# A two-layer encoder in split float32: the gated ConvFFN's convolution and product put off by a few weight units, and more units of the down projection's second chunk ahead of the first chunk's last ones

## The chip, the cores and the metric

One core of a Trainium2 chip runs the whole program. The metric is the device time of one execution in microseconds (us), as the median of several runs. The core has a matrix engine (TensorE, PE in the profile, with its weight loads as PEld), a vector engine (VectorE, DVE), a scalar engine (ScalarE, ACT), a general engine (GpSimd, POOL) and an engine that mainly issues transfers (SyncE, SP; SPq, POOLq and so on are the queues from which transfers are issued).

## The reference

Two layers work on 256 tokens of width 2048 in float32. Layer 0 mixes the tokens with dilated sliding-window attention and differential attention, layer 1 with grouped-query attention and two-dimensional neighbourhood attention. After each mixer comes a gated ConvFFN, and at the end one RMSNorm. The change touches the ConvFFN only:

```
y    = rmsnorm(h, gain)                  # 256 x 2048
gate = y @ w_gate                        # 256 x 5632
up   = y @ w_up                          # 256 x 5632
gate = conv over 3 neighbouring tokens(gate) + bias   # per channel
h    = h + (gelu(gate) * up) @ w_down    # 5632 -> 2048
```

## The kernel before

**Weights.** All weights come from HBM as units of 128 rows x 1024 columns (512 KB). SP issues the load of a unit into one of five `raw` buffers. A product keeps float32 accuracy by three passes: a unit is split into a high part `wh` (a cast on ACT, L234) and a low part `wl` (a subtraction on DVE, L237), and PE multiplies wh by the activation's high part, wl by the high part, and wh by the low part (L198 to L200, L890). There are four `wh` and four `wl` buffers. An ordinary unit is 12 matmuls. Some units go in pairs as blocks, with fewer products: both raw units are loaded (L907, L908), four sums on DVE form new operands (L911, L912, L915, L918), and these are split too; `form` is a fourth operand. The merges at L870 to L875 put the results of the blocks together in the accumulators (`sum`, `gm`, `s`, `tp`).

**ConvFFN.** The 5632 channels are taken in 11 up groups of 512: six in the first half (`HALVES`, groups 0 to 5, `g0 = 0`), five in the second (groups 6 to 10, `g0 = 6`). An up group is two chunks: the gate (x = 0) and the up projection (x = 1). When a chunk's products are done, `done` scales them out of the accumulators into `z` (ACT, L980) and transposes z in squares (DVE, L282). Sixteen transfers of 32 KB then move z to its place in a `qk` tile (L276): four of them are issued by SP and twelve by POOL. When the gate has been moved, `convolved` runs in two parts, each of two 128-channel blocks: a scaled copy on ACT (L1003), two multiply-adds on DVE (L1004, L1006), and a gelu on ACT (L1009). When the up chunk has been moved, `multiplied` forms the product (DVE, L1036) and splits it into `prod`, and for some groups into sums for blocks of the down projection. After each half, the down projection multiplies `prod` by that half's rows of `w_down`: four chunks of 512 columns, taken two and two (c = 0, then c = 2). Their results are added into h (L388), and in the second half squares for the next norm are taken. In layer 1's second half `finish_all` does this.

**What sets the order.** `two_chunks` runs the units of two chunks. `ahead` and `spots` say at which (chunk, unit) the blocks of the next group are loaded. `mixed` changes the order of units: the first chunk stops short of its last `mixed` units, then `mixed` units of the second chunk run, then the first chunk's last ones, then the rest. After every second unit comes a `tick`. `later(delay, fn)` puts fn on a list, and it runs at the tick that is `delay` ticks on; so delays count pairs of weight units. A scheduler then orders the instructions of each engine, by what is ready, in part ahead of their place in the program. Each engine takes its instructions strictly in its own order: what stands behind a waiting instruction waits too.

Of the kernel before, what the change touches and what calls it, by code (L numbers as in the profile page):

```python
# [74 lines left out]
def trunk_kernel(ctx: ExitStack, tc, a, out):  # L75
# [21 lines left out]
    def later(delay, fn, rank=2):  # L97

        pending.append((now[0] + delay, rank, fn))
# [464 lines left out]
    ps = tps("s", 2)  # L564
# [404 lines left out]
    def up_group(layer, j, yT, rstd, prod, ready, ahead, spots, *more):  # L969

        sides = {}

        def hook(x, u):
            if not j and not x and u == 2:
                rstd.append(row_factor())

        def done(x, ps):
            z = new_z("f k")
            for t in range(2):
                S.activation(z.rearrange("p (f t) k -> p t f k", t=2)[:, t],  # L980
                             ps[t].rearrange("p (f k) -> p f k", k=P), AF.Copy, scale=rstd[0][:, t:t + 1])
            sides[x] = quad(2 * x)
            turned(z.rearrange("p b k -> p (b k)"), sides[x].rearrange("p f (t k) -> p (f t) k", k=P), (3,))
            if not x:
                for part in range(2):
                    later(part + 3, lambda part=part: convolved(layer, j, sides, part))

        if not j:
            side[0] = 0
            ready = [[tps("gm", 4), tps("gm", 4)] for _ in range(2)], []  # L990
        nxt = two_chunks([a["up"][layer, j, x] for x in range(2)], yT, 8, ready, ahead, spots, done, hook)
        later(3, lambda: multiplied(j, sides, prod, *more))
        return nxt

    def convolved(layer, j, sides, part):

        if not part:
            sides[2] = quad(4)
        g4, c4 = sides[0], sides[2]
        for i in (2 * part, 2 * part + 1):  # L1000
            f = 4 * j + i
            g, c = g4[:, i, :], c4[:, i, :]
            S.activation(c, g, AF.Identity, scale=convw[:, layer, 1, f:f + 1], bias=convb[:, layer, f:f + 1])  # L1003
            V.scalar_tensor_tensor(c[:, 1:SEQ], g[:, 0:SEQ - 1], convw[:, layer, 0, f:f + 1],  # L1004
                                   c[:, 1:SEQ], op0=ALU.mult, op1=ALU.add)
            V.scalar_tensor_tensor(c[:, 0:SEQ - 1], g[:, 1:SEQ], convw[:, layer, 2, f:f + 1],  # L1006
                                   c[:, 0:SEQ - 1], op0=ALU.mult, op1=ALU.add)
        half = c4[:, 2 * part:2 * part + 2, :]
        S.activation(half, half, AF.Gelu_apprx_tanh)  # L1009
# [34 lines left out]
    def down_front(src, c, act, forms, homes):  # L1044
        return front(src[c:c + 2], act, [2 * n + 1 for n in HALVES[0][2]], forms, homes)

    def ffn(layer, yT, gain, last=False):
        rstd, res, ready = [], None, None
        for g0, g1, seven in HALVES:
            prod, forms = [], {}  # L1050
            nk = 4 * (g1 - g0)
            nu = nk // 2
            src = [a["down"][layer, c, 2 * g0:2 * g1] for c in range(4)]
            for j in range(g0, g1):
                if j + 1 < g1:
                    ahead, spots = (lambda: up_front(layer, j + 1, yT)), [(0, 5 if j == 0 else 3), (1, 5 if j == 0 else 3)]
                    spots = spots[-len(blocks(j + 1)):]
                else:
                    ahead = lambda: down_front(src, 0, prod, forms, ["pt", "pt", "scc"] if g0 else ["act20", "act22", "scc"])
                    spots = [(0, 3), (1, 1), (1, 4)]  # L1060
                ready = up_group(layer, j, yT, rstd, prod, ready, ahead, spots, forms, g0, seven)
            if g0:
                res = [None] * KT
                if last:
                    finish_all(src, prod, forms, nk, ready)
                    return
            for c in (0, 2):
                if not c:
                    ahead, spots = (lambda: down_front(src, 2, prod, forms, ["qk0", "qk2", "qk4"])), [(1, 2), (1, 4), (1, 5)]
                elif not g0:  # L1070
                    ahead, spots = (lambda: up_front(layer, g1, yT)), [(1, 2), (1, 6)]
                else:
                    ahead = None
                ready = two_chunks(src[c:c + 2], prod, nu, ready, ahead, spots, lambda x, ps: finish_chunk(
                    ps, c + x, gain, res, 1 + x if c == 0 else 1), lambda x, u: last_product(c + x, u, nu), 2 if g0 and not c else 0)
        return res

    def last_product(c, u, nu):
        if not c and u == nu - 2:
            flush()  # L1080
# [184 lines left out]
    def finish_all(src, act, forms, nk, ready):  # L1265

        def done(ps, c):
            if not c:
# [5 lines left out]
        nu = nk // 2  # L1274
        load_gains()
        ready = two_chunks(src[0:2], act, nu, ready, lambda: down_front(src, 2, act, forms, ["qk0", "qk2", "qk4"]),
                           [(1, 2), (1, 4), (1, 5)], lambda x, ps: done(ps, x),
                           lambda x, u: last_product(x, u, nu), 2)
        pss, direct = ready[:2]
        for u, s4, t4 in direct:  # L1280
            direct_products(pss, src[2:4], act, u, s4, t4)
# [165 lines left out]
```

## Time and profile before

| | us |
|---|---|
| median of 3 runs | 2431.88 |
| lowest and highest | 2427.51, 2438.07 |
| the profiled execution | 2433.43 |
| its span on the core | 2431.4 |
| PE busy in the span | 2390.6 |
| DVE busy | 1856.6 |
| ACT busy | 1413.3 |
| POOL busy | 540.0 |

The mean granted clock of the profiled execution was 0.998. In its span layer 0's ConvFFN lies at about 660 to 1363 us and layer 1's at about 1715 to 2424 us. A row of the timeline reads: start, duration, engine, line of the kernel, operation, output<-inputs, and in brackets how long the engine was idle before it and what it waited for. A row with x2 stands for two instructions in a row, with the time of both. A row of the waits reads: who waited for whom, us in total, how often, the longest.

### The profile page before, as it was taken

To read this page: it belongs to the slowest core of one execution; us is meant where nothing else is said; L and a number is where in the kernel's file an instruction comes from. 1 tells how busy PE (TensorE), PEld (TensorE's weight loads), DVE (VectorE), ACT (ScalarE), POOL (GpSimd) and SP (SyncE) were. 2 spreads that over 40 slices of the span, in tenths; PEclk is the share of its full clock that TensorE was granted. 3 is DMA by queue.
4 is the path that set the end of the run, shared out by engine and by line. 5 is a ranking of instruction groups with operands and counts; after the bars stand their busy time and mean duration, and the time that the engine had idled before them with its cause. 6 is when DMAs were issued, how large, how long until landed. Compare 5 with 4: busy or idle time off the path is not lost.

```text
span 2431.4 us, 33503 instructions
## 1 busy us (share of the span) xinstructions
PE 2390.6 (98%) x10844; PEld 1972.4 (81%) x10844; DVE 1856.6 (76%) x2525; ACT 1413.3 (58%) x2106; POOL 540.0 (22%) x940
## 2 busy tenths in 40 slices
PE   9999999999999999999999999999999999999998
PEld 7888888888877887788777888888788877888777
DVE  6576567666778997778888667766788977789986
ACT  6455455566656665456666567545566654566654
POOL 1132032321222322012231200322123320033310
PEclk9999999999999999999999999999999999999999
DMA  8678678866777887778888754667688887788875
GB/s 308 202 196 241 198 189 242 222 191 195 214 208 221 250 248 227 228 224 235 246 235 237 239 181 141 193 189 212 189 240 256 236 230 232 224 239 234 246 237 180
DMA packets 296464, 538.19 MB, mean 221 GB/s; under 512 B 160088, under 2 KB 161496, under 8 KB 296288
## 3 DMA queue, kind: packets, MB, share of 16 engines
q1 hardware_dynamic: 265776, 502.66, 66.6%
q0 software_dynamic: 30080, 32.74, 7.8%
q8 instruction: 85, 1.39, 0.2%
q14 instruction: 91, 0.75, 0.1%
q10 hardware_dynamic: 432, 0.66, 0.1%
HBM read 490.99 MB, written 2.18 MB: 203 GB/s over the span
## 4 chain that ended last, share of the span: by engine, by line
PE 68%; DMA 11%; DVE 11%; issue 4%; POOL 2%; ACT 2%; SPq 1%; DVEq 0%; ACTq 0%; POOLq 0%
PE gm L890 15%; PE gm L198 10%; PE gm L199 10%; PE gm L200 10%; PE s L890 9%; PE tp L890 6%; DVE wl L237 5%; DMA qk<-z 5%; DMA raw<-in_down 3%; PE gm L148 2%; DMA raw<-in_up 2%; POOL qk L276 2%; PE gm L153 1%; ACT wh L234 1%; DVE qk L1004 1%
## 5 line engine op out<-in xcount | busy, mean ns | idle before, releaser
L234 ACT CAST wh<-raw 128x1024 fp32r<-128x1024 f32 (+1 forms) x922 | 927.5, 1018 | 695.7 <-PE gm L200 249.8
L237 DVE TENSOR_TENSOR wl<-raw,wh 128x1024 fp32r<-128x1024 f32 (+1 forms) x922 | 1075.8, 1180 | 325.2 <-ACT wh L234 316.5
L276 POOL DMA_DIRECT2D qk<-z x656 | 378.5, 585 | 1148.5 <-DVE z L282 1073.1
L199 PE MATMUL gm<-wl,yT 128*128 128x512 f32 x988 | 385.1, 390 | 1.7 <-DVE wl L237 1.7
L198 PE MATMUL gm<-wh,yT 128*128 128x512 f32 x988 | 386.6, 392 | 0.0
L200 PE MATMUL gm<-wh,yT 128*128 128x512 f32 x988 | 385.0, 390 | 0.0
L890 PE MATMUL gm<-wh,yT 128*128 128x512 f32 x1040 | 332.9, 390 | 0.0
L890 PEld LDWEIGHTS gm<-wh,yT 128*128 128x128 f32 x1040 | 195.5, 188 | 40.9
L199 PEld LDWEIGHTS gm<-wl,yT 128*128 128x128 f32 x988 | 185.7, 188 | 39.5 <-DVE wl L237 2.4
L200 PEld LDWEIGHTS gm<-wh,yT 128*128 128x128 f32 x988 | 185.5, 188 | 39.0
L198 PEld LDWEIGHTS gm<-wh,yT 128*128 128x128 f32 x988 | 185.6, 188 | 37.9 <-ACT junk L268 0.4
L890 PE MATMUL gm<-wl,yT 128*128 128x512 f32 x520 | 203.7, 392 | 2.2 <-DVE wl L237 2.2
L890 PE MATMUL s<-wh,yT 128*128 128x512 f32 x568 | 184.5, 390 | 0.0
L890 PE MATMUL gm<-wh,prod 128*128 128x512 f32 (+1 forms) x560 | 177.8, 389 | 1.0 <-ACT wh L234 1.0
L890 PE MATMUL tp<-wh,yT 128*128 128x512 f32 x496 | 156.3, 389 | 0.0
L890 PEld LDWEIGHTS s<-wh,yT 128*128 128x128 f32 x568 | 106.6, 188 | 22.6
L890 PEld LDWEIGHTS gm<-wh,prod 128*128 128x128 f32 x560 | 105.1, 188 | 22.8 <-ACT wh L234 1.4
L890 PEld LDWEIGHTS gm<-wl,yT 128*128 128x128 f32 x520 | 97.7, 188 | 26.4 <-DVE wl L237 5.5
L890 PE MATMUL gm<-wl,prod 128*128 128x512 f32 x280 | 110.1, 393 | 6.1 <-DVE wl L237 6.1
L890 PE MATMUL s<-wl,yT 128*128 128x512 f32 x284 | 111.0, 391 | 0.4 <-DVE wl L237 0.4
L890 PEld LDWEIGHTS tp<-wh,yT 128*128 128x128 f32 x496 | 93.1, 188 | 19.3
L199 PE MATMUL gm<-wl,mix 128*128 128x512 f32 x256 | 100.6, 393 | 2.0 <-DVE wl L237 2.0
(336 smaller groups left out, 3731.1 us busy)
## 6 DMA issues: line engine op xcount, KB each, us to landing
raw<-in_up SPq DMA_DIRECT2D x390, 512.0 KB, 4.9
raw<-in_down SPq DMA_DIRECT2D x200, 512.0 KB, 4.6
raw<-in_eva_qk SPq DMA_DIRECT2D x96, 512.0 KB, 4.3
raw<-in_eva_v SPq DMA_DIRECT2D x46, 512.0 KB, 6.1
qk<-z POOLq DMA_DIRECT2D x656, 32.0 KB, 4.6
raw<-in_evb_qk SPq DMA_DIRECT2D x32, 512.0 KB, 4.8
raw<-in_ev_out SPq DMA_DIRECT2D x32, 512.0 KB, 4.0
raw<-in_od_qk SPq DMA_DIRECT2D x32, 512.0 KB, 4.0
```

The source lines that it names most:

```text
L148: T.matmul(ps.rearrange("p a b -> p (a b)"), wh[:, k * P:(k + 1) * P], act[u * 8 + k].rearrange("p a b -> p (a b)"), start=(u == 0 and k = ...
L153: T.matmul(ps[:, 1, :], wl[:, k * P:(k + 1) * P], act[u * 8 + k][:, 0, :], start=False, stop=(u * 8 + k == KT - 1))
L198: T.matmul(ps[t], ah, wh[:, sl], start=(kt == 0), stop=False)
L199: T.matmul(ps[t], ah, wl[:, sl], start=False, stop=False)
L200: T.matmul(ps[t], al, wh[:, sl], start=False, stop=(kt == nk - 1))
L234: first = S.copy(dst_h, src)
L237: V.tensor_tensor(dst_l, src, dst_h.bitcast(F32), op=ALU.subtract)
L276: (nc.sync if i in on_sync else G).dma_start(dst[j * 32:(j + 1) * 32, :, i * 32:(i + 1) * 32], z[i * 32:(i + 1) * 32].rearrange("p (b j c) ...
L890: T.matmul(ps, x, y, start=first and i == 0, stop=last and i == 2, skip_group_check=onto)
L1004: V.scalar_tensor_tensor(c[:, 1:SEQ], g[:, 0:SEQ - 1], convw[:, layer, 0, f:f + 1], c[:, 1:SEQ], op0=ALU.mult, op1=ALU.add)
```

## The change

Five numbers change:

1. `convolved` runs one tick later (`part + 4` ticks after the gate chunk in place of `part + 3`), and in the first group (j = 0) two ticks later.
2. `multiplied` runs one tick later (4 in place of 3).
3. In the first half, the third block of the down projection's second pair of chunks is loaded one unit later: spot (1, 6) in place of (1, 5).
4. `mixed` for the first pair of down chunks is 2 in the first half (it was 0) and 4 in the second (it was 2).
5. The same 4 in place of 2 in `finish_all`, for layer 1's second half.

```diff
             if not x:
                 for part in range(2):
-                    later(part + 3, lambda part=part: convolved(layer, j, sides, part))
+                    later(part + (4 if j else 5), lambda part=part: convolved(layer, j, sides, part))
...
         nxt = two_chunks([a["up"][layer, j, x] for x in range(2)], yT, 8, ready, ahead, spots, done, hook)
-        later(3, lambda: multiplied(j, sides, prod, *more))
+        later(4, lambda: multiplied(j, sides, prod, *more))
...
                 if not c:
-                    ahead, spots = (lambda: down_front(src, 2, prod, forms, ["qk0", "qk2", "qk4"])), [(1, 2), (1, 4), (1, 5)]
+                    ahead, spots = (lambda: down_front(src, 2, prod, forms, ["qk0", "qk2", "qk4"])), [(1, 2), (1, 4), (1, 5 if g0 else 6)]
...
                 ready = two_chunks(src[c:c + 2], prod, nu, ready, ahead, spots, lambda x, ps: finish_chunk(
-                    ps, c + x, gain, res, 1 + x if c == 0 else 1), lambda x, u: last_product(c + x, u, nu), 2 if g0 and not c else 0)
+                    ps, c + x, gain, res, 1 + x if c == 0 else 1), lambda x, u: last_product(c + x, u, nu), 0 if c else 4 if g0 else 2)
...
                            [(1, 2), (1, 4), (1, 5)], lambda x, ps: done(ps, x),
-                           lambda x, u: last_product(x, u, nu), 2)
+                           lambda x, u: last_product(x, u, nu), 4)
```

Every engine keeps the same instructions; what changes is their order. On PE and POOL the up groups keep theirs. Three places, in the names of the program (a number tells buffers apart; the same work can have another number in the two kernels):

Layer 0, the boundary of groups 0 and 1. ACT, before and then after: `wh<-raw` are casts of weight units, `qk<-qk,convb,convw` is the convolution's first step on the gate of group 0, `sum` and `s` are merges.

```order
L234 CAST wh_6421<-raw_6419 128x1024
L1003 ACTIVATE qk_6437<-qk_6272,convb,convw 128x256 x2
L234 CAST wh_6447<-raw_6445 128x1024
L234 CAST wh_6465<-raw_6463 128x1024
L1009 ACT_TABLE_LOAD
L1009 ACTIVATE qk_6437<-qk_6437 128x512
L870 COPY sum_6481<-s_6380 128x512
L1003 ACTIVATE qk_6437<-qk_6272,convb,convw 128x256 x2
L234 CAST wh_6520<-raw_6518 128x1024
```

```order
L234 CAST wh_6421<-raw_6419 128x1024
L1003 ACTIVATE qk_6554<-qk_6272,convb,convw 128x256
L234 CAST wh_6439<-raw_6437 128x1024
L870 COPY sum_6473<-s_6380 128x512
L234 CAST wh_6457<-raw_6455 128x1024
L234 CAST wh_6505<-raw_6503 128x1024
L1003 ACTIVATE qk_6554<-qk_6272,convb,convw 128x256 x3
L874 COPY s_6381<-sum_6475 128x512
L234 CAST wh_6520<-raw_6518 128x1024
```

The first step of the convolution stays behind the cast of wh_6421, but it stands there once in place of twice; the other three follow after three more casts, and the gelu behind them.

The same boundary on DVE, before and then after: `wl<-raw,wh` are the low parts of weight units, `qk<-qk,convw,qk` the convolution's multiply-adds.

```order
L237 TENSOR_TENSOR wl_6422<-raw_6419,wh_6421 128x1024
L1004 SCALAR_TENSOR_TENSOR qk_6437<-qk_6272,convw,qk_6437 128x255
L1006 SCALAR_TENSOR_TENSOR qk_6437<-qk_6272,convw,qk_6437 128x255
L1004 SCALAR_TENSOR_TENSOR qk_6437<-qk_6272,convw,qk_6437 128x255
L1006 SCALAR_TENSOR_TENSOR qk_6437<-qk_6272,convw,qk_6437 128x255
L237 TENSOR_TENSOR wl_6448<-raw_6445,wh_6447 128x1024
L237 TENSOR_TENSOR wl_6466<-raw_6463,wh_6465 128x1024
L871 TENSOR_TENSOR sum_6482<-sum_6481,tp_6382 128x512
L1004 SCALAR_TENSOR_TENSOR qk_6437<-qk_6272,convw,qk_6437 128x255
L872 TENSOR_TENSOR sum_6483<-sum_6482,s_6381 128x512
```

```order
L237 TENSOR_TENSOR wl_6422<-raw_6419,wh_6421 128x1024
L1004 SCALAR_TENSOR_TENSOR qk_6554<-qk_6272,convw,qk_6554 128x255
L1006 SCALAR_TENSOR_TENSOR qk_6554<-qk_6272,convw,qk_6554 128x255
L237 TENSOR_TENSOR wl_6440<-raw_6437,wh_6439 128x1024
L871 TENSOR_TENSOR sum_6474<-sum_6473,tp_6382 128x512
L237 TENSOR_TENSOR wl_6458<-raw_6455,wh_6457 128x1024
L872 TENSOR_TENSOR sum_6475<-sum_6474,s_6381 128x512
L873 TENSOR_TENSOR tp_6382<-sum_6474,tp_6383 128x512
L875 TENSOR_TENSOR tp_6383<-sum_6475,tp_6383 128x512
L237 TENSOR_TENSOR wl_6506<-raw_6503,wh_6505 128x1024
L237 TENSOR_TENSOR wl_6521<-raw_6518,wh_6520 128x1024
L1004 SCALAR_TENSOR_TENSOR qk_6554<-qk_6272,convw,qk_6554 128x255
```

Ahead of the first weight split behind wl_6422, four multiply-adds have become two; the others follow after four splits.

SP at the end of layer 1's second half's up groups, before and then after: `in_up` and `in_down` are weight units, `qk<-z` the four of the sixteen moves that SP issues.

```order
L131 DMA raw_21007<-in_up 128x1024
L131 DMA raw_21025<-in_up 128x1024
L907 DMA raw_21043<-in_down 128x1024
L276 DMA qk_20919<-z_20916 32x8x32 x4
L908 DMA raw_21044<-in_down 128x1024
L131 DMA raw_21078<-in_up 128x1024
L131 DMA raw_21096<-in_up 128x1024
```

```order
L131 DMA raw_21007<-in_up 128x1024
L131 DMA raw_21025<-in_up 128x1024
L907 DMA raw_21043<-in_down 128x1024
L908 DMA raw_21044<-in_down 128x1024
L276 DMA qk_20898<-z_20895 32x8x32 x4
L131 DMA raw_21078<-in_up 128x1024
L131 DMA raw_21096<-in_up 128x1024
```

The block's second load (L908) has passed the four moves of the gate.

DVE at that end, where the last group but one is multiplied (L1036), before and then after.

```order
L237 TENSOR_TENSOR wl_20844<-raw_20841,wh_20843 128x1024
L237 TENSOR_TENSOR wl_20862<-raw_20859,wh_20861 128x1024
L1036 TENSOR_TENSOR qk_20683<-qk_20683,qk_20694 128x1024
L237 TENSOR_TENSOR wl_20880<-raw_20877,wh_20879 128x1024
L332 TENSOR_TENSOR sums_20897<-qk_20683 128x128
L334 TENSOR_TENSOR sums_20897<-qk_20683 128x128
L333 TENSOR_TENSOR sums_20897<-sums_20897,qk_20683 128x128
L237 TENSOR_TENSOR prod_20904<-qk_20683,prod_20904 128x256
L335 TENSOR_TENSOR sums_20897<-qk_20683,sums_20897 128x128
L237 TENSOR_TENSOR prod_20907<-qk_20683,prod_20907 128x256
L237 TENSOR_TENSOR prod_20910<-qk_20683,prod_20910 128x256
L237 TENSOR_TENSOR prod_20913<-qk_20683,prod_20913 128x256
```

```order
L237 TENSOR_TENSOR wl_20837<-raw_20834,wh_20836 128x1024
L237 TENSOR_TENSOR wl_20862<-raw_20859,wh_20861 128x1024
L911 TENSOR_TENSOR t_3953_20938<-raw_20934 128x512
L237 TENSOR_TENSOR wl_20880<-raw_20877,wh_20879 128x1024
L237 TENSOR_TENSOR wl_20919<-raw_20916,wh_20918 128x1024
L912 TENSOR_TENSOR raw_20934<-raw_20935,raw_20934 128x512
L1036 TENSOR_TENSOR qk_20770<-qk_20770,qk_20686 128x1024
L915 TENSOR_TENSOR raw_20935<-raw_20935,t_3953_20938 128x512
L237 TENSOR_TENSOR wl_20942<-raw_20934,wh_20941 128x1024
L918 TENSOR_TENSOR raw_20935<-raw_20935 128x512
L237 TENSOR_TENSOR wl_20944<-raw_20935,wh_20943 128x512
L237 TENSOR_TENSOR wl_20944<-t_3953_20938,wh_20943 128x512
```

L1036, which waits for the moves of the up chunk, has come behind more weight splits and into the sums of a block; the product's own sums and splits now follow behind the block's splits.

## The prediction

> **What bounds the kernel now.** I read the page's busy line first, then a table of stretches, then the waits, then the timeline at each place where TensorE (PE) stands still. The busy line:
>
> ```profile
> PE 2390.6 (98%) x10844; PEld 1972.4 (81%) x10844; DVE 1856.6 (76%) x2525; ACT 1413.3 (58%) x2106; POOL 540.0 (22%) x940
> ```
>
> PE is busy in 2390.6 of 2431.4 us. The change adds and removes no matmul, so it can only win from the 40.8 us in which PE is idle. The two ConvFFNs, by stretches (length, then busy time of PE, PEld, DVE, ACT and POOL):
>
> ```profile
> 660.00:1363.00 703.00, 688.72 (x3000) 561.37 (x3000) 583.00 (x759) 415.73 (x566) 161.41 (x280) 1.00 0.79 234
> 1715.00:2424.00 709.00, 695.15 (x3032) 565.56 (x3030) 582.16 (x760) 413.40 (x564) 154.50 (x268) 1.00 0.77 230
> ```
>
> PE idles 703.00 - 688.72 = 14.3 us in the first and 709.00 - 695.15 = 13.9 us in the second. The other 12.7 us lie outside the code that the change touches. So 28.1 us are the most that there is to win. Cut closer, with one row for each place where PE stops (length minus PE's busy time is the idle time):
>
> ```profile
> 695.00:715.00 20.00, 18.66 (x81) 14.76 (x80) 15.71 (x22) 12.57 (x18) 1.48 (x3) 1.00 0.62 198
> 750.00:765.00 15.00, 12.20 (x46) 9.33 (x45) 11.54 (x17) 9.51 (x14) 2.78 (x5) 0.89 0.57 188
> 915.00:940.00 25.00, 23.91 (x104) 18.88 (x103) 21.11 (x27) 15.64 (x22) 6.29 (x12) 1.00 0.81 243
> 960.00:985.00 25.00, 22.60 (x99) 17.97 (x98) 21.55 (x28) 9.71 (x13) 0.00 (x0) 1.00 0.67 209
> 1165.00:1200.00 35.00, 33.64 (x147) 27.04 (x146) 31.81 (x48) 21.52 (x33) 11.52 (x21) 1.00 0.73 212
> 1250.00:1290.00 40.00, 37.88 (x159) 29.11 (x158) 37.41 (x53) 24.95 (x37) 11.52 (x20) 1.00 0.79 219
> 1310.00:1340.00 30.00, 26.84 (x115) 21.02 (x114) 27.85 (x38) 18.49 (x30) 4.61 (x8) 1.00 0.76 223
> 1740.00:1760.00 20.00, 18.04 (x78) 14.20 (x77) 16.29 (x23) 13.49 (x19) 3.35 (x6) 1.00 0.58 168
> 1790.00:1805.00 15.00, 14.21 (x62) 11.37 (x61) 12.49 (x19) 9.52 (x14) 1.97 (x4) 1.00 0.65 215
> 1940.00:1985.00 45.00, 40.87 (x173) 31.67 (x172) 37.68 (x50) 27.39 (x38) 10.11 (x19) 1.00 0.79 233
> 2010.00:2025.00 15.00, 13.45 (x59) 10.82 (x59) 12.02 (x17) 6.55 (x9) 0.00 (x0) 1.00 0.61 202
> 2230.00:2240.00 10.00, 9.61 (x43) 7.59 (x42) 8.81 (x13) 7.22 (x11) 2.55 (x5) 1.00 0.65 215
> 2270.00:2330.00 60.00, 56.91 (x243) 44.64 (x242) 52.53 (x72) 38.18 (x55) 17.55 (x31) 1.00 0.83 247
> 2355.00:2375.00 20.00, 18.15 (x79) 14.10 (x78) 18.48 (x25) 11.89 (x18) 0.00 (x0) 1.00 0.63 195
> ```
>
> These are seven sites in each layer, in order: **A** the boundary of up groups 0 and 1 (1.34 and 1.96 us), **B** of groups 1 and 2 (2.80, 0.79), **C** the end of the first half's up groups (1.09, 4.13), **D** the first half's down phase (2.40, 1.55), **E** the first boundary of the second half (1.36, 0.39), **F** the end of its up groups (2.12, 3.09), **G** its down phase (3.16, 1.85). Together 28.0 us. At all other group boundaries PE does not stop.
>
> Who is late there? PE waits for weight splits (L237 on DVE, some L234 on ACT), and the splits stand behind instructions that wait for data (line waited for, us in total, times, longest):
>
> ```profile
> ACT qk L1003 <- DMA qk<-z: 32.1, 16, 4.3
> DVE raw L912 <- DMA raw<-in_down: 20.1, 12, 4.5
> DVE qk L1036 <- DMA qk<-z: 15.0, 12, 3.4
> ```
>
> The convolution's first step (L1003) and the product (L1036) wait for the moves of the transposed z, and the block sums (L912) for a down weight.
>
> **The change, part by part.** No instruction comes or goes; every cost is one of place.
>
> *Sites A and B: a split ahead of the rest of the convolution.* Site A and then site B in the first layer:
>
> ```profile
> 699.17 1.09 ACT L1003 ACTIVATE qk<-qk,convb,convw 128x256 f32<-128x256 f32 x2 [4.06 <-DMA qk<-z]
> 699.81 0.48 DVE L1004 SCALAR_TENSOR_TENSOR qk<-qk,convw,qk 128x255 f32<-128x255 f32 x1 [3.43 <-ACT qk L1003]
> 701.65 2.36 DVE L237 TENSOR_TENSOR wl<-raw,wh 128x1024 fp32r<-128x1024 f32 x2
> 702.92 0.50 PE L199 MATMUL gm<-wl,yT 128*128 128x512 f32 x1 [0.55 <-DVE wl L237]
> ...
> 752.78 1.09 ACT L1003 ACTIVATE qk<-qk,convb,convw 128x256 f32<-128x256 f32 x2 [5.95 <-DMA raw<-in_up]
> 755.29 1.03 ACT L234 CAST wh<-raw 128x1024 fp32r<-128x1024 f32 x1
> 756.37 0.51 PE L890 MATMUL gm<-wh,form 128*128 128x512 f32 x1 [1.13 <-ACT wh L234]
> 757.28 3.49 DVE L237 TENSOR_TENSOR wl<-raw,wh 128x1024 fp32r<-128x1024 f32 x3
> 758.55 0.49 PE L890 MATMUL gm<-wl,form 128*128 128x512 f32 x1 [1.68 <-DVE wl L237]
> ```
>
> At A, the first L1003 keeps its place and its wait, but only one stands ahead of the next cast (two took 1.09 us, so about 0.55 earlier), and two steps of the convolution instead of four ahead of the next split. Four of them fill 699.81 to 701.65, so two are worth 0.9 us. That is more than the 0.55 us that PE waits, and the 0.79 behind it (1.34 - 0.55) stands behind the second pair, which now has three splits ahead of it. I take A from 1.34 to 0, and from 1.96 to 0.3 in the second layer, where the first stop is longer.
> At B the cast of 755.29 comes two L1003 earlier, at about 754.4: 1.13 becomes 0.3. Its split comes behind four convolution steps instead of eight, and may start when its cast ends, at 755.5 instead of 757.28: 1.8 us earlier against 1.68 of wait. So B goes from 2.80 to 0.3, and from 0.79 to 0.
> What is late next: group 0's product L1036 now stands one split earlier. It waits on DVE for the up quarter's moves, and the split behind it waits with it. The longest such wait on the moves is 3.4 us. I charge 1.2 us in the first layer and 0.7 in the second.
>
> *Sites C and F: the block's second load ahead of the moves.* The second layer's C:
>
> ```profile
> 1956.77 2.55 SPq L276 DMA_DIRECT2D qk<-z  x4
> 1959.43 0.54 SPq L908 DMA_DIRECT2D raw<-in_down  x1
> 1965.81 0.69 DVE L912 TENSOR_TENSOR raw<-raw,raw 128x512 f32<-128x512 f32 x1 [4.48 <-DMA raw<-in_down]
> 1967.76 0.50 PE L890 MATMUL gm<-wh,prod 128*128 128x512 f32 x1 [1.02 <-ACT wh L234]
> 1969.14 0.50 PE L890 MATMUL gm<-wl,prod 128*128 128x512 f32 x1 [0.88 <-DVE wl L237]
> ```
>
> SP issues the four moves only when z is transposed, and the load L908 stands behind them; DVE waits 4.48 us for it, and PE 1.02 + 0.88 us for the splits behind it. After the change L908 is issued ahead of the moves, some 3 to 4 us earlier, so these 1.90 us go. The product L1036 stands two splits and a block sum later, which takes off an estimated 0.5 us, and the rest, 1.7 us, stays. C: 1.09 to 0.1, 4.13 to 1.7. At F a like load is waited for, and a first L1003 behind which a split waits now has that split ahead of it: 2.12 to 0.5, 3.09 to 1.0.
>
> *Sites D, E and G: the order of the down units.* Two (first half) or four (second half) units of the second chunk come ahead of the first chunk's last two (now four), so the last products are needed 2 units later on PE, which is just the extra delay given to L1036: no gain for it there. The stops at D and G stand behind block sums whose loads are late, and these load earlier only in the second half. I take a fifth off: D 2.40 to 1.9 and 1.55 to 1.2, G 3.16 to 2.5 and 1.85 to 1.5. At E the splits stand behind one of the twelve waits of L1036, which is now put off by two units: 1.36 to 0.3, 0.39 to 0.
>
> *The quiet boundaries* lose their order too: convolution steps and block sums alternate, and some splits come up to one convolution step (0.48 us) later. One example of the cover:
>
> ```profile
> 843.57 2.35 DVE L237 TENSOR_TENSOR wl<-raw,wh 128x1024 fp32r<-128x1024 f32 x2
> 846.94 0.39 PE L890 MATMUL gm<-wl,form 128*128 128x512 f32 x1
> ```
>
> The first of the two splits ends near 844.79 and PE needs it at 846.94, 2.15 us later. So one step costs nothing there; I charge 0.8 us in all for places with less cover.
>
> **Sum.** A 0.3, B 0.3, C 1.8, D 3.1, E 0.3, F 1.5, G 4.0: 11.3 us of 28.0 stay, a gain of 16.7. Less 1.9 for group 0's product and 0.8 for the quiet boundaries: 14.0. The moves land when z is ready plus their own time, and PE that runs ahead meets the next landing earlier; no row prices that, so its bounds are 0 and the whole gain. The trace has about as many stops that hang on landings as stops that hang on mere order, but the convolution also comes two units later; I take a quarter, 3.5 us. The net gain is 10.5 us. The profiled execution took 2433.43 us, so it becomes 2422.9; the median of the runs, 1.55 lower, becomes **2421 us**, 0.43% less.
>
> **Rivals.**
> *Nearly all stops vanish.* For it: a later convolution waits less for moves, and at A to C and F mere order explains most. Against it: D and G keep their late loads. Idle left 3 to 4 us: 2431.9 - 25 = 2407.
> *Nothing is won on balance.* The first L1003 of group 0 keeps its place and wait, and L908 ahead of the moves may delay them. The down loads (count, KB each, median us from issue to landing):
>
> ```profile
> raw<-in_down SPq DMA_DIRECT2D x200, 512.0 KB, 4.6
> ```
>
> If the moves land later by what such a load takes (the median of 4.6 us), the convolution at C and F waits instead of L912, and the gains of C and F (1.0 + 2.4 + 1.6 + 2.1 = 7.1 us) return as new stops; with half of the rest given back at later landings, 2.4 to 3.5 us remain: about 2429.
> The Trainium skill, "DMA: Bandwidth & Descriptors", section "Queues, rings and completion order", speaks for this rival: a semaphore increment lands only after every earlier write from that DMA engine, across its queues, so by that rule the four moves are not seen as done before the load ahead of them has landed. No row here separates the two; by it C and F would win nothing.
> *Slower.* One mechanism: the transposition L282 stands behind more interleaved work on DVE at the ends of the groups, the moves land later, and L1036, now with its splits behind it, waits on DVE at the ten boundaries that are quiet now. The price is the longest wait seen, 4.3 us, less the 2.15 us of cover: 2.15 at ten places, 21.5 us; with the 10.5 us won elsewhere kept, 2443, without them 2453. It decides where the moves land over 5.3 us later (two units, by which the convolution is put off, of 12 matmuls at 2390.6 / 10844 = 0.22 us each). Against it: the interleaved steps are 0.4 to 0.7 us each.
> *The change does not do what it says* at some sites, because the order is set by what is ready: at A the first L1003 indeed stays. That is held in the second rival.
>
> **Chances.** Forecast 0.48 (2414 to 2428 on its own), nearly all vanish 0.15, nothing won 0.27, slower 0.10. A measurement of this kernel can hardly tell less than 0.5% (12.2 us) from no change. Faster by more: all of the first rival and nearly half of the forecast (10.5 us is just short of the bound), 0.15 + 0.23 = 0.38. Slower by more: most of the last rival, 0.09. Within: 0.53. The range runs from the first rival's time to a little above no change, 2407 to 2437.
>
> **What would show it.** Right: in the profile after, PE is busy for the same 2390 us with 17 to 18 us idle in the two stretches instead of 28; L912's wait of 4.48 us at the half's end is gone; sites A and B show stops under 0.5 us; D and G keep most of theirs. Wrong: L1003 or L1036 wait longer for qk<-z in total than 32.1 and 15.0 us (the second rival, if at the half ends; the slower one, if at quiet boundaries), or new stops of PE of over 1 us stand between 770 and 910 or between 1200 and 1250.

## The result: 0.5% slower

Over twelve runs of each, the kernel before takes 2428.8 us (median) and the changed kernel 2442.89 us. The ratio is 1.0052, with a 95% interval of 1.0039 to 1.0065. 2421 was forecast, so even the sign was wrong, and the time lies outside the range. The profiled execution after took 2447.4 us with a span of 2445.6 us, 14.2 us more than before. The busy line of the page after:

```profile
PE 2396.8 (98%) x10844; PEld 1969.6 (81%) x10844; DVE 1853.2 (76%) x2525; ACT 1410.4 (58%) x2106; POOL 537.9 (22%) x940
```

The instructions are the same in number on every engine. DVE and ACT do a little less busy time than before, and PE is busy 6.2 us more with the same matmuls; the last section comes back to that.

Where did the time come from? The windows of two stretches that were quiet before, groups 2 to 4 in each layer; first of the kernel before, then of the changed one (length, then busy time and count of PE, PEld, DVE, ACT, POOL):

```profile
775.00:905.00 130.00, 130.00 (x574) 107.33 (x573) 120.39 (x167) 87.11 (x123) 41.49 (x72) 1.00 0.84 251
1815.00:1940.00 125.00, 124.95 (x549) 102.41 (x549) 113.88 (x160) 81.12 (x116) 41.30 (x72) 1.00 0.82 242
```

```profile
775.00:905.00 130.00, 126.11 (x544) 100.85 (x543) 115.39 (x163) 81.49 (x117) 41.36 (x72) 1.00 0.80 235
1815.00:1940.00 125.00, 122.55 (x531) 98.72 (x530) 107.70 (x151) 77.34 (x111) 37.96 (x67) 1.00 0.82 242
```

In 130 us PE ran 574 matmuls before and 544 after: the quiet boundaries are not quiet any more. To have it for all places, the start of the n-th matmul in one trace can be held against the start of the n-th in the other, since the up groups have the same matmuls in the same order. The time between two such matmuls, after less before, summed over the places of both layers:

```
                 forecast   measured (us)
A, B               -4.4        -5.0
quiet boundaries   +0.8       +20.2
C, E, F            -8.6        -1.6
D, G               -1.9        +0.4
given back         +3.5
all the rest                   -0.1
sum               -10.6       +13.9
```

A and B won about what was forecast. The loss is at the boundaries that were priced at 0.8 us, and C and F didn't win.

How does a split come late there? The waits after, of the instructions that the prediction named and of one that it did not (a form cast on ACT that waits for the block's last sum, L918); then that row before:

```profile
ACT qk L1003 <- DMA qk<-z: 63.0, 19, 5.6
ACT form L234 <- DVE raw L918: 54.0, 42, 2.6
...
DVE qk L1036 <- DMA qk<-z: 25.7, 14, 2.9
DVE raw L912 <- DMA raw<-in_down: 7.9, 11, 1.5
```

```profile
ACT form L234 <- DVE raw L918: 17.8, 17, 2.2
```

Two waits have grown, both on ACT: L1003 for the moves from 32.1 to 63.0 us, and the form cast for L918 from 17.8 to 54.0 us. The timeline of the boundary of groups 3 and 4 in layer 0 shows what stands behind them, in the changed kernel:

```profile
841.89 0.60 ACT L1003 ACTIVATE qk<-qk,convb,convw 128x256 f32<-128x256 f32 x1 [2.56 <-DMA qk<-z]
842.40 1.03 ACT L234 CAST wh<-raw 128x1024 fp32r<-128x1024 f32 x1
843.46 1.22 DVE L237 TENSOR_TENSOR wl<-raw,wh 128x1024 fp32r<-128x1024 f32 x1 [3.35 <-ACT wh L234]
844.74 0.50 PE L890 MATMUL gm<-wl,form 128*128 128x512 f32 x1 [0.75 <-DVE wl L237]
...
848.42 1.24 DVE L282 STREAM_TRANSPOSE z<-z 128x1024 f32<-128x1024 f32 x1
849.58 2.32 DVE L237 TENSOR_TENSOR wl<-raw,wh 128x1024 fp32r<-128x1024 f32 x2
850.82 0.50 PE L890 MATMUL gm<-wl,yT 128*128 128x512 f32 x1 [0.64 <-DVE wl L237]
...
852.82 0.69 DVE L915 TENSOR_TENSOR raw<-raw,t 128x512 f32<-128x512 f32 x1
853.42 0.48 DVE L1004 SCALAR_TENSOR_TENSOR qk<-qk,convw,qk 128x255 f32<-128x255 f32 x1
853.81 1.82 DVE L237 TENSOR_TENSOR wl<-raw,wh 128x1024 fp32r<-128x1024 f32 x2
855.55 0.69 DVE L237 TENSOR_TENSOR wl<-t,wh 128x512 fp32r<-128x512 f32 x1
856.15 0.69 DVE L918 TENSOR_TENSOR raw<-raw 128x512 f32<-128x512 f32 x1
856.87 0.62 ACT L234 CAST form<-raw 128x512 fp32r<-128x512 f32 x1 [2.06 <-DVE raw L918]
857.40 1.04 ACT L234 CAST wh<-raw 128x1024 fp32r<-128x1024 f32 x1
858.47 1.23 DVE L237 TENSOR_TENSOR wl<-raw,wh 128x1024 fp32r<-128x1024 f32 x1 [0.26 <-ACT wh L234]
859.75 0.50 PE L890 MATMUL gm<-wl,yT 128*128 128x512 f32 x1 [0.42 <-DVE wl L237]
```

and in the kernel before, where the four first steps stand in a row behind one more cast, and the sum L918 right behind the other sums, ahead of the block's splits:

```profile
839.47 1.06 ACT L234 CAST wh<-raw 128x1024 fp32r<-128x1024 f32 x1 [0.17 <-PE tp L890]
841.25 2.08 ACT L1003 ACTIVATE qk<-qk,convb,convw 128x256 f32<-128x256 f32 x4 [0.73 <-DMA qk<-z]
...
852.27 0.69 DVE L915 TENSOR_TENSOR raw<-raw,t 128x512 f32<-128x512 f32 x1
852.99 0.69 DVE L918 TENSOR_TENSOR raw<-raw 128x512 f32<-128x512 f32 x1
853.60 1.82 DVE L237 TENSOR_TENSOR wl<-raw,wh 128x1024 fp32r<-128x1024 f32 x2
854.30 0.62 ACT L234 CAST form<-raw 128x512 fp32r<-128x512 f32 x1
```

After, ACT takes a first step of the convolution ahead of the cast. It waits 2.56 us for the moves; the cast behind it, the split on DVE behind that and PE wait in turn. Some 6 us on, PE stops for 0.64 us for two splits that stand behind multiply-adds and the transposition L282. Further on, L918 stands behind a multiply-add and three of the block's splits, so the form cast waits 2.06 us, and the next unit's cast waits behind it on ACT.

The first step has moved ahead of a cast at six boundaries (3 and 4, 4 and 5, 9 and 10 in both layers), and a stop of 0.63 or 0.64 us stands some 9 us behind it at each. L918 has moved behind three splits at all 14 boundaries behind B inside a half, and the form cast waits 2.1 us at each. The product L1036, which also waits longer (25.7 us against 15.0), stands ahead of four late splits: 1.5 of the 12.7 us that PE is idle at these places.

### The profile page after: what moved, and what is told of

It is laid out like the page before. It is cut to its first block, busy times and chain, and to the rows that moved or that the text cites. A ratio compares the mean times of both kernels' runs of the same rounds, so it can differ in the third digit from the quotient of the medians.

```text
span 2445.6 us, 33468 instructions
## 1 busy us (share of the span) xinstructions
PE 2396.8 (98%) x10844; PEld 1969.6 (81%) x10844; DVE 1853.2 (76%) x2525; ACT 1410.4 (58%) x2106; POOL 537.9 (22%) x940
## 5 line engine op out<-in xcount | busy, mean ns | idle before, releaser
L890 PEld LDWEIGHTS s<-wh,yT 128*128 128x128 f32 x568 | 106.7, 188 | 22.2
```

The source lines that it names most:

```text
L890: T.matmul(ps, x, y, start=first and i == 0, stop=last and i == 2, skip_group_check=onto)
```

## The experiments

The theory after this comparison: what costs is the new order at the quiet boundaries, mainly by these two waits. The rivals: the down projection's order, and being later as such. Each ratio is to the kernel before on the same chip, with its 95% interval.

**One part of the change at a time.** Four kernels: both delays alone, the down projection's part alone, the convolution's delay alone, the product's delay alone.

```diff
# delays: convolution part + (4 if j else 5), product 4; the rest as before
# down: spot (1, 6) and mixed 2 / 4 / 4; both delays 3 as before
# convonly: convolution part + (4 if j else 5); the rest as before
-        later(3, lambda: multiplied(j, sides, prod, *more))     # multonly: this alone
+        later(4, lambda: multiplied(j, sides, prod, *more))
```

> Only the two delays are changed (convolution +1 tick, +2 in group 0; product +1); the down projection's order of units and its block's spot are as before. Theory (order at the quiet boundaries): the loss comes from convolution steps that now stand between and ahead of weight splits in the up groups, so nearly all of the 14 us stays: 11 to 16 us over the kernel before, with some 20 short stops of PE of 0.2 to 0.8 us between 800 and 915, 1200 and 1260, 1850 and 1955 and 2250 and 2310 us. Rival (the down projection's order): the loss comes from units of the second chunk ahead of the first chunk's last ones, so that this kernel is at 0 to 5 us over before, or faster than it by the 5 us that sites A and B won.

> Only the down projection is changed (2 and 4 units of the second chunk ahead, the block's spot one unit later); the delays are as before. Theory (order at the quiet boundaries): within 3 us of the kernel before, and no stop at boundaries that were quiet. Rival (the down projection's order): 8 to 14 us over before, with the stops in the down phases, at about 960 to 1000, 1300 to 1360, 2010 to 2050 and 2355 to 2420 us.

> Only the convolution is later (+1 tick, +2 in group 0); product and down projection as before. On DVE its steps then alternate with the block sums, as in the changed kernel; on ACT its first step stays behind the cast at the quiet boundaries. Theory (order at the quiet boundaries, by the steps between block sums): 5 to 11 us over before, with the stops behind the block's splits (0.4 to 0.65 us), and without those of 0.7 us behind the convolution's first step. Rival (the wait for the moves ahead of a cast on ACT is the whole cost): within 3 us of before, since that step is behind its cast here, or faster by what sites A and B won.

> Only the product is later (+1 tick); convolution and down projection as before. On ACT two first steps of the convolution then stand ahead of a cast at quiet boundaries where none did. Theory (steps between block sums): 0 to 5 us over before, one stop of 0.3 to 1 us at those boundaries. Rival (the wait for the moves ahead of a cast on ACT is the whole cost): 8 to 14 us over before, from stops of 0.7 us and more behind casts that wait with the convolution's first step.

Measured: both delays 2445.65 us, ratio 1.0051 (1.0036 to 1.0066), the whole loss; the down projection 2434.78 us, 1.0015 (1.0002 to 1.0029); the convolution's delay 2440.69 us, 1.0034 (1.0023 to 1.0045); the product's delay 2436.01 us, 1.0011 (1.0000 to 1.0023). All four lie within the theory's numbers (13.8, 2.9, 8.8 and 4.1 us over the kernel before). The rival of the down projection falls, and so does the one by which L1003's wait is the whole cost. The two waits in the kernel with the convolution's delay alone:

```profile
ACT form L234 <- DVE raw L918: 57.4, 39, 2.6
ACT qk L1003 <- DMA qk<-z: 37.4, 16, 5.3
```

and with the product's delay alone:

```profile
ACT qk L1003 <- DMA qk<-z: 57.3, 20, 5.6
ACT form L234 <- DVE raw L918: 14.9, 18, 1.4
```

Each delay brings one of the two waits, with its change of order: the convolution's delay alone has L918 behind three splits at the same 14 boundaries, the product's delay alone has the first step one cast earlier at the same six. At the quiet boundaries the first kernel loses 7.8 us, the second 0.3, both delays together 18.5 (by the table below). So the wait of L1003 costs next to nothing there by itself, and the two cost more together: the stops of 0.6 us behind the transposition stand in the kernels with both delays alone. Probably the first wait has used up the cover of the splits by then; this wasn't measured apart. Over the whole kernel the medians don't show it, as they just add up (8.8 and 4.1 us against 13.8). That the product's delay moves L1003 at all is the scheduler's doing: the product's program says nothing of that step.

**The first step kept at its place.** The scheduler had hoisted L1003 ahead of its place in the program. One edit on the changed kernel keeps it there:

```diff
-            S.activation(c, g, AF.Identity, scale=convw[:, layer, 1, f:f + 1], bias=convb[:, layer, f:f + 1])
+            tc.keep_in_program_order(S.activation(c, g, AF.Identity, scale=convw[:, layer, 1, f:f + 1], bias=convb[:, layer, f:f + 1]))
```

At the same quiet boundary ACT then has this order; in the changed kernel (left) the first step stood ahead of the second cast:

```
changed                                        first step kept
L234 CAST wh<-raw                              L234 CAST wh<-raw
L874 COPY gm<-sum                              L874 COPY gm<-sum
L1003 ACTIVATE qk<-qk,convb,convw              L234 CAST wh<-raw
L234 CAST wh<-raw                              L234 CAST wh<-raw
L1003 ACTIVATE qk<-qk,convb,convw x3           L980 ACTIVATE z<-tp,rstd
L234 CAST wh<-raw                              L980 ACTIVATE z<-tp,rstd
L980 ACTIVATE z<-tp,rstd                       L234 CAST wh<-raw
L980 ACTIVATE z<-tp,rstd                       L1003 ACTIVATE qk<-qk,convb,convw x2
L234 CAST wh<-raw                              L234 CAST wh<-raw
```

> The changed kernel, with the convolution's first step (L1003, ACT) kept at its place in the program, so that the scheduler doesn't hoist it: at a quiet boundary it now stands behind two more casts, in two pairs, and its steps on DVE come in fours, away from the block sums. Theory (the loss is the order at the quiet boundaries: form casts that wait for L918 behind convolution steps, 54 us in total against 18 before, and casts behind a first step that waits for its moves, 63 us against 32): both waits fall back to 25 us or less, the short stops go, and the kernel is 10 to 20 us under the changed one, 2423 to 2433. Rival (being later is itself the cost, since the product then waits for its gelu and the moves land late): no better than the changed kernel, 2440 to 2448, with L1036 waiting over 40 us in total.

Measured: 2398.34 us, ratio 0.9880 (0.9867 to 0.9892): 1.2% faster than the kernel before and some 1.7% (1.0052 / 0.9880) faster than the changed one, well beyond what was expected. Its busy line, the same two windows and the form cast's wait:

```profile
PE 2377.3 (99%) x10844; PEld 1974.4 (82%) x10844; DVE 1853.3 (77%) x2525; ACT 1424.8 (59%) x2106; POOL 539.0 (22%) x940
```

```profile
775.00:905.00 130.00, 130.00 (x573) 107.36 (x573) 119.79 (x164) 86.90 (x121) 41.36 (x72) 1.00 0.82 246
1815.00:1940.00 125.00, 125.00 (x552) 103.22 (x551) 114.84 (x158) 82.31 (x116) 41.36 (x72) 1.00 0.83 245
```

```profile
ACT form L234 <- DVE raw L918: 5.2, 10, 1.4
```

PE stops nowhere in these stretches, and one wait of L1003 for the moves is left in the trace, of 0.6 us. L918 is back right behind the other sums at these boundaries, too, so this edit takes both changes of order away and doesn't tell them apart. The rival, that being later is itself the cost, falls: with the order kept, later is the gain. The next kernel shows that from the other side.

**The first step kept, the old delays.** The same edit on the kernel before.

> The kernel before, with the convolution's first step (L1003, ACT) kept at its place in the program and all delays as before. At the quiet boundaries two of the four first steps then stand behind three more casts. Theory (each split that stands ahead of a convolution step that waits or works is a gain): 0 to 6 us under the kernel before. Rival (the scheduler's own order is the better one where delays are short, and the gain of the kept order comes only with the longer delays): 0 to 5 us over before.

Measured: 2418.39 us, ratio 0.9965 (0.9953 to 0.9977), a gain of 9 us (2427.53 - 2418.39), a little over what was expected. On the same chip the change as a whole is thus worth 2418.39 - 2398.34 = 20 us, if L1003 is kept at its place; without that it costs 14.

**DVE's half of that order alone.** The changed kernel with the multiply-adds (L1004, L1006) kept in place, and L1003 free. DVE's order at the quiet boundaries is then nearer to that of the kernel with L1003 kept, though some multiply-adds still alternate with the sums, while ACT has four first steps in a row, ahead of a cast.

```diff
-            V.scalar_tensor_tensor(c[:, 1:SEQ], g[:, 0:SEQ - 1], convw[:, layer, 0, f:f + 1],
-                                   c[:, 1:SEQ], op0=ALU.mult, op1=ALU.add)
+            tc.keep_in_program_order(V.scalar_tensor_tensor(c[:, 1:SEQ], g[:, 0:SEQ - 1], convw[:, layer, 0, f:f + 1],
+                                   c[:, 1:SEQ], op0=ALU.mult, op1=ALU.add))
...
```

> The changed kernel, with the convolution's multiply-adds (L1004, L1006, DVE) kept at their place in the program, while its first step (L1003, ACT) is left to the scheduler, which puts all four in a row ahead of a cast, two casts earlier than in the kernel with L1003 kept. Theory (what costs is the multiply-adds between and ahead of the splits and the block's last sum): as fast as the kernel with L1003 kept, 2396 to 2406. Rival (what costs is a first step that waits for its moves ahead of a cast on ACT): the wait of L1003 for the moves stays at 30 us or more, and the time is 2412 to 2435.

Measured: 2424.5 us, ratio 0.9965 (0.9952 to 0.9977). Half of the way from 1.0052 to 0.9880: the theory's number falls, and the rival's holds. The waits:

```profile
ACT qk L1003 <- DMA qk<-z: 39.7, 19, 4.8
ACT form L234 <- DVE raw L918: 21.1, 21, 2.5
```

The quiet boundaries lose 0.2 us here, but neither change of order is left there: L1003 stands as far back as in the kernel before, and L918 behind no split. What this kernel still loses against the kernel with L1003 kept is spread (by the table below 12.1 us at C, E and F, 5.1 at D and G, 3.9 at the quiet boundaries, 3.1 at A and B). At C and F a first step stands one to three casts earlier than in the kernel before, and waits 2.1 to 3.6 us for the moves. The two kernels also differ a little in DVE's order, so L1003's wait ahead of a cast is the likely cause there, and not a shown one.

**The block sums kept at their place.** The changed kernel with L911, L912, L915 and L918 in program order.

```diff
-        V.tensor_tensor(w21, w21, w22, op=ALU.subtract)
+        tc.keep_in_program_order(V.tensor_tensor(w21, w21, w22, op=ALU.subtract))
...
```

> The changed kernel, with the four block sums (DVE) kept at their place in the program. The fourth form's cast on ACT then stands behind the next unit's cast, not ahead of it, and the convolution's first step behind its cast at the quiet boundaries; the convolution's steps still alternate with the block sums. Theory (a form cast that waits for L918 holds the next unit's cast behind it): 6 to 12 us under the changed kernel, few stops behind blocks. Rival (the convolution's steps on DVE themselves delay the splits): within 4 us of the kernel with only the convolution later, 2437 to 2445, with the stops of 0.4 to 0.65 us still there.

Measured: 2437.5 us, ratio 1.0040 (1.0026 to 1.0055). By the total the rival was right. By place it was not: the quiet boundaries lost nothing (-0.1 us), A and B won 10.7, and all of the loss, 23.4 us, is at D and G, where keeping the sums in order changes the down phase too. The multiply-adds still alternate with the sums, but L918 stands behind one split in place of three, the form cast behind the next unit's cast, and the first step at the quiet boundaries where it stood before:

```profile
ACT qk L1003 <- DMA qk<-z: 29.8, 17, 4.3
ACT form L234 <- DVE raw L918: 12.8, 22, 0.6
```

So at the quiet boundaries the alternation costs nothing by itself; the cost goes with the two changes of order. No kernel moved L918 alone, so what each of them costs rests on the kernels with one delay. The edit brought a second change with it, and its total says little.

**Only groups 0 and 1 later.** The kernel before with `part + (5 if j == 0 else 4 if j == 1 else 3)`.

> The kernel before, with the later convolution for groups 0 and 1 only (+2 and +1 ticks, in each layer's first half); the product, all other groups and the down projection as before. Sites A and B get the changed order, the quiet boundaries keep theirs. Theory: 1 to 6 us under the kernel before, since A and B win what they won in the changed kernel's profile (5.7 us in both layers) and nothing is lost elsewhere. Rival (the gain of A and B in single profiles is chance: in the kernel with both delays they won 2.6 us, in the one that leaves the up groups alone 0): within 2 us of the kernel before.

Measured: 2428.1 us, ratio 1.0003 (0.9994 to 1.0012): no change, as the rival had it. Its profile shows 3.3 us won at A and B, and 2.6 us lost at the boundaries behind them.

**What the other parts are worth once the order is kept.** Three kernels beside the one with L1003 kept: without the down projection's part; with the product at its old delay of 3 (the convolution as in the change, so two ticks later in group 0, where the expectation says one); with the product at 5.

> The kernel with L1003 kept, but with the down projection's order of units and its block's spot as before the change. It tells what the down projection's part of the change is worth once the up groups are quiet. Theory (the last product then comes too late for the first chunk's last units, which the second chunk's units give time for): 3 to 10 us slower than with that part (2398), stops of 1 to 3 us in the down phases at D and G. Rival (that part is worth nothing): within 2 us of 2398.

> The kernel with L1003 kept and the convolution later by one tick in all groups, but the product at its old delay of 3; the down projection as in the change. It tells what the later product is worth. Theory (the product stands where it stood, since it waits for the gelu anyway): within 2 us of the kernel with both (2398). Rival (an earlier product waits for the last gelu and the moves, ahead of a split): 3 to 10 us slower.

> The kernel with L1003 kept and all of the change, the product later by one more tick (5). Theory (no stop is left in the up groups for it to take away; only the down phases feel it, where the last product comes later): 0 to 6 us slower than 2398. Rival (the stops that are left, 0.3 to 1.6 us at seven places, hang on the product): 1 to 4 us faster.

Measured: 2401.13 us, ratio 0.9869 (0.9852 to 0.9887); 2404.3 us, 0.9890 (0.9873 to 0.9907); 2405.08 us, 0.9890 (0.9872 to 0.9909). All three intervals hold 0.9880, so none of these parts can be told from nothing, not even the down projection's: its theory of 3 to 10 us falls. These three ran on another chip than the kernel with L1003 kept, so only the ratios compare, and the expectations of within 2 us can't be decided.

The time between the same matmuls, less that of the kernel before, in the profiles of these kernels (us):

```
                                      A,B  quiet  C,E,F    D,G   rest    all
changed                              -5.0   20.2   -1.6    0.4   -0.1   13.9
both delays alone                    -2.1   18.5   -2.8    0.1   -1.8   11.8
convolution's delay alone            -2.3    7.8    5.8   -0.8   -1.8    8.8
product's delay alone                 2.1    0.3    0.4    2.2   -2.3    2.6
down projection alone                 0.0    0.4   -1.8    0.7   -2.3   -3.0
groups 0 and 1 alone                 -3.3    2.6   -1.5   -1.1   -3.7   -6.9
changed, multiply-adds kept          -7.6    0.2   -3.3    3.0    0.5   -7.2
changed, block sums kept            -10.7   -0.1   -5.3   23.4   -3.3    4.1
changed, first step kept            -10.7   -3.7  -15.4   -2.1   -3.9  -35.8
  same, down projection as before   -10.7   -3.7  -11.7   -3.2   -2.0  -31.2
  same, product at 3                -10.7   -2.9  -13.9   -0.5   -1.8  -29.7
  same, product at 5                -10.7   -3.4  -11.4    0.1   -2.9  -28.4
before, first step kept              -3.2   -0.8   -5.8   -2.1   -3.4  -15.3
```

Each row is one execution. The column "rest", where all kernels have the same order, differs by up to 4 us, and the sums stray from the medians by several us (groups 0 and 1 alone: -6.9 here, no change in twelve runs). So only differences well above that are read from it. The borders between the places are drawn by hand, and single entries hang on them: with E counted by its own stops (1165 to 1200 and 2225 to 2245 us of the kernel before), and other borders a few us elsewhere, the changed kernel loses 19.6 us at the quiet boundaries and wins 1.0 at C, E and F; the kernels with one delay lose 10.8 (convolution) and 1.9 (product) at the quiet boundaries, that with both 16.6, and the kernel with L1003 kept wins 1.2 there and 17.9 at C, E and F.

## Why the prediction was wrong

*What bounds the kernel* was right: the time lies in stops of PE for weight splits behind waiting work. The kernel with L1003 kept shows it, since it does the same work and gets rid of nearly all of these stops in the up groups. The bound of 28.1 us was wrong, though: that kernel's span is 35.5 us shorter (2431.4 - 2395.9). The last section says why.

*Sites A and B*, forecast -4.4 us with group 0's product, measured -5.0 in this profile. The working held, though B differs between profiles by some us: with both delays alone, which has the same order there, A and B won only 2.1. What the working left out is the clock: the prediction's own row for B has 0.89 of it, and the last section says what that is worth; so it is in part luck that 5.0 lies so near to 4.4.

*The quiet boundaries* are the step that failed. They were charged 0.8 us for "up to one convolution step" of delay on DVE against 2.15 us of cover. Measured: 20.2 us. The sentence on ACT is missing there: the order had, at six of these boundaries, a first step of the convolution moved ahead of a cast, and, at all, a form cast that waits for a sum put behind three splits. A cast is short; what was not priced is that ACT's whole queue stands while the instruction at its head waits, 2.06 and 2.56 us in the rows above, about the whole cover of 2.15 us. How the 20.2 us divide between the two changes stays open in part, since they cost more together than apart. At site A the same change on ACT was read and priced; for the quiet boundaries, where no stop stood before, the prediction has no row of ACT. Its own sign of being wrong came: L1003 waited 63.0 us for the moves against 32.1, and L1036 25.7 against 15.0. No new stop there was over 1 us, though: the longest between 770 and 910 us is 0.75.

*Sites C, E and F* were forecast at -8.6 us and gave -1.6. L912's wait fell from 20.1 to 7.9 us in total, so the load ahead of the moves did what was said. A new wait took its place, as at the second layer's C in the changed kernel:

```profile
1972.30 0.69 DVE L912 TENSOR_TENSOR raw<-raw,raw 128x512 f32<-128x512 f32 x1
...
1981.65 0.60 ACT L1003 ACTIVATE qk<-qk,convb,convw 128x256 f32<-128x256 f32 x1 [4.94 <-DMA qk<-z]
1983.24 0.49 PE L890 MATMUL tp<-wh,yT 128*128 128x512 f32 x1 [0.68 <-ACT wh L234]
```

L912 doesn't wait, but a first step of the convolution waits 4.94 us with a cast behind it. That is the outcome of the second rival, by another mechanism (last section). With L1003 kept, these places win 15.4 us. E is misread in the prediction: its stops (at 1170, 1192 and 2234 us in the kernel before) aren't at the second half's first boundary, but follow the product of group 7 or stand at the boundary of groups 8 and 9.

*Sites D and G*: -1.9 forecast, +0.4 measured, and the down projection's part alone is at 1.0015. The estimate of a fifth had nothing behind it in the trace, and no run shows a gain from this part.

*The rivals.* The slower one had 0.10. Its place was right, ten boundaries that were quiet, and its price of 21.5 us is close to the 20.2 measured there. That its time of 2443 us is the one measured is luck, since it kept 10.5 us of gains elsewhere, of which this profile shows 6.3. Its mechanism was not right: it named L1036, behind which stand 1.5 of the 12.7 us of idle time at these places, and it needed moves that land 5.3 us later, which no row here shows. L1003 and the form cast did most of it. *That the change doesn't do what it says* was set aside too quickly: the delay asked for a later convolution, and at six boundaries the scheduler put its first step one cast earlier instead (the kernel with the product's delay alone does so too, that with the convolution's doesn't). Why it places it there wasn't tried.

## What to carry to other kernels

A delay in the program is a wish where a scheduler orders the queues: look at every place where the order changed, not only at those that stop now, and for each ask what stands behind an instruction that waits for a transfer on an in-order engine. If a change that should help loses, keep the moved instruction at its place before giving the change up: here the same edit was worth +14 us without that and -20 us with it. The idle time of the bounding engine in the profile can understate what its stops cost; count how many of its instructions pass in a stretch.

## What the runs showed of the hardware

A stop of PE costs more than the idle time that the rows show. At site A, in the kernel before:

```profile
701.98 0.39 PE L198 MATMUL gm<-wh,yT 128*128 128x512 f32 x1
702.92 0.50 PE L199 MATMUL gm<-wl,yT 128*128 128x512 f32 x1 [0.55 <-DVE wl L237]
703.25 0.40 PE L200 MATMUL gm<-wh,yT 128*128 128x512 f32 x1
```

While PE runs without a stop, matmuls start every 130.00 / 574 = 0.23 us (the quiet window above), but a row is 0.39 us long, so it overlaps the next. Here two starts lie 702.92 - 701.98 = 0.94 us apart, 0.71 over 0.23, and the next 0.33, 0.10 over: 0.81 us are lost, of which 0.55 show as idle. Over the whole program the same 10844 matmuls are busy 2390.6 us before, 2396.8 after and 2377.3 with L1003 kept, as there are more or fewer stops. With L1003 kept, idle time falls by 22.2 us (from 40.8 to 18.6) and busy time by 13.3, together the 35.5: that is how the gain could exceed 28.1 us.

A longer stop costs clock as well. At B in layer 0 of the kernel before, after stops of 1.13 and 1.68 us, the granted clock was 0.50 from 759.6 to 763.0 us, which is some 1.7 us of work lost in time that counts as busy. So it went in all six profiles in which PE stood still for 1.9 us or more there, for 3.4 us or, in one, 6.8; in the eight with 1.2 us or less the clock stayed at 1.00. The changed kernel stopped 0.76 us there, that with both delays alone 1.23 and 0.76: some 1.7 of the 5.0 us that A and B won is this clock, which the other kernel with the same order didn't win.

The second rival's mechanism did not show. The issues of the second layer's C, about 1950 to 1975 us in the kernel before, where the load follows the moves, and about 1962 to 1982 us in the changed one, where it goes ahead (KB each, median us to landing):

```profile
qk<-z POOLq DMA_DIRECT2D x12, 32.0 KB, 6.8
qk<-z SPq DMA_DIRECT2D x4, 32.0 KB, 2.3
```

```profile
qk<-z POOLq DMA_DIRECT2D x12, 32.0 KB, 6.3
qk<-z SPq DMA_DIRECT2D x4, 32.0 KB, 2.4
```

SP's four moves take 2.4 us against 2.3, though a load of 512 KB is issued 1.8 us ahead of them (the rows of SP have 1965.93 and 1967.76 us). The Trainium skill, "DMA: Bandwidth & Descriptors", section "Queues, rings and completion order", has a semaphore increment land only after every earlier write from the same DMA engine. These rows don't refute that: the load landed 3.4 us after its issue, at about 1969.35 us, and a move that is issued at 1967.76 and takes 2 us or more lands behind it. But what the prediction made of it, moves that are seen 4.6 us later, didn't happen here.
